# Three layer norms in two phases, with the mean's row applied before the reciprocal deviation's, and eight bridge tiles instead of seven

## The chip, the cores and the metric

The kernel runs on one core of one Trainium2 chip. The metric is the device time of one execution in microseconds (us): median of three runs before the change 1218.24 us (1216.67 to 1220.58). Besides, one execution was taken by the hardware profiler; its rows are the ones quoted here.

## What is computed

A whole network of two blocks on 256 tokens of width 1024, in float32. The first block is a mixer of a state-space branch (S5) and an mLSTM, a cross attention and a convolutional feed-forward part (FFN), with RMS norms. The second block has two layers, and it holds the layer norms of this case:

```python
def second_block(x, ...):
    alpha = (2 * DEPTH_2) ** 0.25
    for l in range(DEPTH_2):
        i = l // 2
        if l % 2 == 0:
            y = even_mixer(x, ...)
        else:
            y = odd_mixer(x, ...)
        x = layer_norm(alpha * x + y, ln_g[l, 0], ln_b[l, 0])
        y = conv_ffn(x, ffn_w_up[l], ffn_conv_w[l], ffn_conv_b[l], ffn_w_down[l])
        x = layer_norm(alpha * x + y, ln_g[l, 1], ln_b[l, 1])
    return x
```

Of its four layer norms, three feed matrix products (the FFN of the first layer, the odd mixer, the FFN of the second layer) and go through the function `layer_norm` of the kernel; the fourth is the output and has a function of its own, `last_norm`.

## The kernel before, in words

Activations lie feature-major: a tensor of [128, 8, 256] holds 1024 features as eight groups of 128 partitions, with the 256 tokens along the free axis. A matrix product of such a tensor (`fm_mm`, lines 324 to 330) makes one output tile of 128 features: for each of the eight groups three matmuls, because each float32 operand is split into a high and a low part in the reduced type float32r (high times high, high times low, low times high). So a tile is 24 matmuls of 256 columns. Each weight tile comes through `wload` (lines 312 to 322): a DMA of 512 KB into a buffer `raw`, a cast to `hi` on ScalarE (line 320), and `lo = raw - hi` on VectorE (line 321).

The sums over features that a norm needs are matmuls with a column of ones (line 454) into the one PSUM buffer of pool `pm` (tag "m"). Rows are made from such columns by `row_bcast` (lines 495 to 499): one small matmul against the identity per 128 tokens, into the same buffer "m", which ScalarE then copies to SBUF.

Since a norm takes time, TensorE is bridged. `raw_scaled` (line 526) splits z times g, not normalised, into high and low parts (`xh`, `xl`) with g and b as two more columns, and the first `NRAW` = 7 output tiles (`NROD` = 7 in the odd layer) are multiplied with that. Each such tile needs a PSUM bank for itself (258 columns): four of tag "a" and three of tag "g", which is all there is beside "m". Later `fix` (lines 1072 to 1081) corrects each tile to the product of the normalised rows: with r the reciprocal deviation and rn = -mean x r as rows, it is product x r + (W g) x rn + W b, where W g and W b are the tile's last two columns, copied by line 1076 to `wgb`. After the bridge tiles, TensorE takes the normalised rows `nh` and `nl` (in the odd layer `oh` and `ol`).

The norm itself (`layer_norm`, lines 1044 to 1064): statistics, mean and r as columns by `ln_rstd` (ScalarE lines 1035 and 1036, GpSimd lines 1038 to 1041, which ends with a power), mean x r on GpSimd (line 1050), a broadcast of r and rn in one go (line 1051), a copy of both rows on ScalarE (line 1053). Then, for five pieces of one or two groups: rn x g + b on ScalarE (line 1061), z x g x r on VectorE (line 1062), their sum (line 1063), the cast to the high part on ScalarE (line 515), the low part on VectorE (line 516).

The order of each engine's instructions is made by a scheduler that goes by priorities and a simulated timeline (`schedule_with_timeline_sim`). Norm work has `LPRI` = 600 places of priority over its place in the program, weight loads have `WPRI` = 300; `fix` and the evacuations behind it have none. Each engine then works in that fixed order and waits by semaphores.

Behind the bridge, the FFN (`ffn`, line 594) works in pairs of tiles; its PSUM tiles come from a ring of the four "a" and three "g" buffers. With seven bridge tiles the fourth pair is mixed: one bridge tile and one of normalised rows in another bank "a" (lines 363 to 384).

Of the kernel before, what the change touches and what calls it, by code (L numbers as in the profile page):

```python
# [14 lines left out]
AF = mybir.ActivationFunctionType  # L15
# [5 lines left out]
P = 128  # L21
S = 256
# [7 lines left out]
LAM_INIT = 0.8 - 0.6 * math.exp(-0.3 * 0)  # L30
MAGIC = 12582912.0
WPRI = 300
NRAW = 7
NRMS = 12
ORDER = ("kv0 ks q c0 tm ckv c1 CS0 CS1 CO0 CS2 CO1 CS3 CO2 kr CO3 cq uk uv uq DS0 DS1 DO0 DS2 DO1 DS3 "
         "DO2 DO3").split()
# [222 lines left out]
def _program(ctx, tc, nc, a, offs, dump):  # L259
    V, ACT, G, PE = nc.vector, nc.scalar, nc.gpsimd, nc.tensor  # L260
# [8 lines left out]
    tp = pool(ctx, "tp", 2)  # L269
    sm = pool(ctx, "sm", 4)  # L270
    dr = pool(ctx, "dr", 1, space=DRAM)
    pg = pool(ctx, "pg", 3, space=PSUM)
    pa = pool(ctx, "pa", 4, space=PSUM)
# [3 lines left out]
    def T(pl, shape, tag, dt=F32, **k):  # L277
        cnt[0] += 1
        return pl.tile(list(shape), dt, tag=tag, name="%s_%d" % (tag, cnt[0]), **k)

    mult, add, sub = ALU.mult, ALU.add, ALU.subtract
    stt = V.scalar_tensor_tensor
    tt = V.tensor_tensor
    ts = V.tensor_scalar
    act = ACT.activation
# [13 lines left out]
    def bc(ap, shape):  # L299
        return ap.to_broadcast(list(shape))  # L300
# [194 lines left out]
    def row_bcast(cols, at=None):  # L495
        rb = T(*(at or (pm,)), [P, len(cols) * P], "g" if at else "m")
        for j, c in enumerate(cols):
            mm(rb[:, j * P:(j + 1) * P], bc(c, [P, P]), ident, start=True, stop=True)
        return rb
# [13 lines left out]
    def split(src, h, l, scale=None):  # L513
        if scale is None:
            ACT.copy(h, src)
            tt(l, src, h, op=sub)  # L516
        else:
            act(h, src, AF.Copy, scale=scale)
            stt(l, src, scale, h, op0=mult, op1=sub)
# [68 lines left out]
    def bc2(rs):  # L588
        return bc(rs[:, None, :], [P, 2, S])

    def act_split():
        return T(hp, [P, 8, S], "xh", F32R), T(hp, [P, 8, S], "xl", F32R)
# [434 lines left out]
    def ln_stats(z):  # L1027
        with tc.high_priority(LPRI):
            st = T(pm, [P, 4], "m")
            col_sums(st, [folded(*tiles(z, 8)), folded(*squares(z, 8))])  # L1030
        return st

    def ln_rstd(st):
        nmu, mq = T(sm, [P, 2], "lnmu"), T(sm, [P, 2], "lnmq")
        act(nmu, st[:, 0:2], AF.Copy, scale=-1.0 / D)
        act(mq, st[:, 2:4], AF.Copy, scale=1.0 / D, bias=1e-5)
        var = T(sm, [P, 2], "lnv")
        G.tensor_tensor(var, nmu, nmu, op=mult)
        G.tensor_tensor(var, mq, var, op=sub)
        r = T(sm, [P, 2], "lnr")  # L1040
        G.tensor_tensor(r, var, mhalf[:, :2], op=ALU.pow)
        return nmu, r

    def layer_norm(z, g, b, h, l, xn, pl, tr_="lnrow", tf="fx"):
        st = ln_stats(z)
        raw = raw_scaled(z, g, b, S + 2)
        with tc.high_priority(LPRI):
            nmu, r = ln_rstd(st)
            nr = T(sm, [P, 2], "lnn")
            G.tensor_tensor(nr, nmu, r, op=mult)  # L1050
            rb = row_bcast([r[:, 0:1], r[:, 1:2], nr[:, 0:1], nr[:, 1:2]])
            rs = T(pl, [P, 2, S], tr_)
            ACT.copy(rs.rearrange("p a s -> p (a s)"), rb)
            rr, rn = rs[:, 0], rs[:, 1]
            for k, w in ((0, 1), (1, 1), (2, 2), (4, 2), (6, 2)):
                s2 = slice(k, k + w)
                f = T(tp, [P, w, S], "sqa", bufs=2)
                u = T(tp, [P, w, S], "sq", bufs=3)
                for n in range(w):
                    c = k + n  # L1060
                    act(f[:, n, :], rn, AF.Identity, scale=g[:, c:c + 1], bias=b[:, c:c + 1])  # L1061
                    stt(u[:, n, :], z[:, c, :], g[:, c:c + 1], rr, op0=mult, op1=mult)
                tt(xn[:, s2, :], u, f, op=add)
                split(xn[:, s2, :], h[:, s2, :], l[:, s2, :])

        places = iter([(pa, "a")] * 4 + [(pg, "g")] * 3)

        def banks(n):
            raw["tiles"] -= n
            return [T(pl_, [P, raw["n"]], tag) for pl_, tag in (next(places) for _ in range(n))]  # L1070

        def fix(rps):
            f = T(pl, [P, 2, S], tf, bufs=2)
            for n in range(len(rps)):
                wgb = T(sm, [P, 2], "wgb")
                V.tensor_copy(wgb, rps[n][:, S:S + 2])
                act(f[:, n, :], rn, AF.Identity, scale=wgb[:, 0:1], bias=wgb[:, 1:2])
                t = T(tp, [P, S], "sq", bufs=3)
                tt(t, rps[n][:, 0:S], rr, op=mult)
                tt(f[:, n, :], f[:, n, :], t, op=add)  # L1080
            return f

        raw.update(fix=fix, banks=banks, tiles=NRAW if tf == "fx" else NROD)
        return raw

    def last_norm(z):
        gb = T(hp, [P, 2, D], "xh")
        nc.scalar.dma_start(gb, bass.AP(a["ln_last"].tensor, 0, [[0, P], [D, 2], [1, D]]))
        u = T(hp, [P, 2, D], "xl")
        o = T(xp, [P, 2, D], "x")  # L1090
        st = ln_stats(z)
        zt = [[T(pa, [P, 512], "a") for q in range(2)] for t in range(2)]

        def turn(k):
            for t in range(2):
                PE.transpose(zt[t][k // 4][:, (k % 4) * P:(k % 4 + 1) * P], z[:, k, t * P:(t + 1) * P], ident)

        for k in range(6):
            turn(k)
        with tc.high_priority(LPRI):  # L1100
            nmu, r = ln_rstd(st)
        for k in range(6, 8):
            turn(k)
        for t in range(2):
            for q in range(2):
                c = slice(512 * q, 512 * q + 512)
                stt(u[:, t, c], zt[t][q], nmu[:, t:t + 1], gb[:, 0, c], op0=add, op1=mult)
        for t, c0, n in ((0, 0, 512), (0, 512, 512), (1, 0, 512), (1, 512, 256), (1, 768, 256)):
            c = slice(c0, c0 + n)
            stt(o[:, t, c], u[:, t, c], r[:, t:t + 1], gb[:, 1, c], op0=mult, op1=add)  # L1110
            nc.sync.dma_start(a["out"][t * P:(t + 1) * P, c], o[:, t, c])
# [497 lines left out]
    with ExitStack() as ph:  # L1609
# [22 lines left out]
        rs, rc = rms_defer(x, 8, C["mix_norm_g"], 1e-6, xh, xl)  # L1632
# [100 lines left out]
    h, l = act_split()  # L1733
    rs, rc = rms_defer(x3, 8, C["final_norm_g"], 1e-6, h, l)
# [10 lines left out]
    with ExitStack() as ph:  # L1745
# [12 lines left out]
        z = T(xp, [P, 8, S], "x")  # L1758
        gemm_pairs("ev_out", range(4), 6, yh, yl, join=True, **residual_a(xa, z))
    for i in range(2):  # L1760
# [4 lines left out]
        if i == 1:  # L1765
            with ExitStack() as ph:
# [6 lines left out]
                h, l = T(ap_, [P, 8, S], "oh", F32R), T(ap_, [P, 8, S], "ol", F32R)  # L1773
                raw = norm_od(h, l, ap_, "ockv", "csb0")
                yh, yl = odd(ap_, h, l, W, KO, raw)
                z = T(xp, [P, 8, S], "x")
# [3 lines left out]
        z = T(xp, [P, 8, S], "x")  # L1780
# [3 lines left out]
        if i == 0:  # L1784
            xa = T(xp, [P, 8, S], "x")
            norm_od = norm(1, z, xa)
    last_norm(z)


# [10 lines left out]
```

## Time and profile before

| what | value |
|---|---|
| median of three runs | 1218.24 us (1216.67 to 1220.58) |
| the profiled execution's own time | 1222.49 us |
| its span, first to last instruction | 1220.7 us |
| mean granted TensorE clock | 0.98 of full speed |
| busy share of the span | TensorE 96%, VectorE 74%, ScalarE 56%, GpSimd 8% |

In the profile, PE is TensorE's matmuls, PEld its weight loads, DVE is VectorE, ACT ScalarE, POOL GpSimd, SP the engine that issues most DMAs. Lines such as L321 are lines of the kernel; many operations have the line of a helper. Matmuls overlap, so a count of matmuls started in a stretch says more than the busy time of PE. PEclk is the TensorE clock that was granted: 1.00 is 2.4 GHz, 0.50 is 1.2 GHz, and a value between is a mix of both in the stretch. The three norms lie at about 660 to 702 us (first FFN), 855 to 897 us (odd mixer) and 1010 to 1047 us (second FFN).

### The profile page before, as it was taken

To read this page: it belongs to the slowest core of one execution; us is meant where nothing else is said; L and a number is where in the kernel's file an instruction comes from. 1 tells how busy PE (TensorE), PEld (TensorE's weight loads), DVE (VectorE), ACT (ScalarE), POOL (GpSimd) and SP (SyncE) were. 2 spreads that over 40 slices of the span, in tenths; PEclk is the share of its full clock that TensorE was granted. 3 is DMA by queue.
4 is the path that set the end of the run, shared out by engine and by line. 5 is a ranking of instruction groups with operands and counts; after the bars stand their busy time and mean duration, and the time that the engine had idled before them with its cause. 6 is when DMAs were issued, how large, how long until landed. Compare 5 with 4: busy or idle time off the path is not lost.

```text
span 1220.7 us, 23603 instructions
## 1 busy us (share of the span) xinstructions
PE 1175.4 (96%) x9370; PEld 1111.6 (91%) x9370; DVE 905.4 (74%) x1744; ACT 681.7 (56%) x1205; POOL 94.5 (8%) x94
## 2 busy tenths in 40 slices
PE   7779999999999999999999899999999999999997
PEld 7769989999999999899998899998977789999986
DVE  8998957866689886667564886666687758976654
ACT  5345564755566765446355675554675566755541
POOL 4830000100000000000001000001000001000010
PEclk9979999999999999999999899999998999999998
DMA  7423445664356556656423556566754215666561
GB/s 262 139 87 114 147 137 179 205 202 157 100 177 196 183 177 181 196 175 215 163 79 106 170 173 187 176 181 190 261 182 139 70 54 193 208 188 188 160 201 36
DMA packets 61276, 199.41 MB, mean 163 GB/s; under 512 B 8502, under 2 KB 12398, under 8 KB 60910
## 3 DMA queue, kind: packets, MB, share of 16 engines
q1 hardware_dynamic: 54864, 191.60, 49.5%
q10 hardware_dynamic: 6302, 6.32, 1.6%
q8 instruction: 73, 1.20, 0.4%
q14 instruction: 37, 0.30, 0.1%
HBM read 196.28 MB, written 1.60 MB: 162 GB/s over the span
## 4 chain that ended last, share of the span: by engine, by line
PE 82%; DVE 11%; ACT 2%; DMA 2%; issue 2%; SPq 0%; DVEq 0%; ACTq 0%
PE g L329 10%; PE g L328 10%; PE g L330 10%; PE a L328 7%; PE a L329 7%; PE a L330 7%; PE a L393 5%; PE g L393 4%; DVE lo L321 3%; PE a L395 3%; PE g L337 2%; PE g L339 2%; PE g L338 2%; PE g L395 2%; PE a L947 1%
## 5 line engine op out<-in xcount | busy, mean ns | idle before, releaser
L321 DVE TENSOR_TENSOR lo<-raw,hi 128x1024 fp32r<-128x1024 f32 (+3 forms) x359 | 431.2, 1206 | 180.7 <-ACT hi L320 178.0
L320 ACT CAST hi<-raw 128x1024 fp32r<-128x1024 f32 (+3 forms) x359 | 363.7, 1020 | 355.4 <-PE g L329 138.8
L328 PE MATMUL g<-xh,hi 128*128 128x256 f32 (+1 forms) x616 | 176.2, 287 | 7.9 <-ACT xh L568 7.6
L329 PE MATMUL g<-xl,hi 128*128 128x256 f32 (+1 forms) x624 | 178.9, 287 | 0.3 <-DVE xl L569 0.3
L330 PE MATMUL g<-xh,lo 128*128 128x256 f32 (+1 forms) x616 | 176.3, 287 | 2.7 <-DVE lo L321 2.7
L328 PE MATMUL a<-nh,hi 128*128 128x256 f32 x560 | 159.9, 286 | 4.6 <-ACT sqa L1061 2.7
L329 PE MATMUL a<-nl,hi 128*128 128x256 f32 x560 | 159.5, 285 | 0.9 <-DVE nl L516 0.9
L330 PE MATMUL a<-nh,lo 128*128 128x256 f32 x560 | 159.3, 285 | 0.0
L328 PEld LDWEIGHTS g<-xh,hi 128*128 128x128 f32 x616 | 117.7, 191 | 9.9 <-ACT xh L568 7.9
L330 PEld LDWEIGHTS g<-xh,lo 128*128 128x128 f32 x616 | 117.4, 191 | 4.4 <-DVE lo L321 3.4
L329 PEld LDWEIGHTS g<-xl,hi 128*128 128x128 f32 x624 | 119.0, 191 | 1.4 <-DVE xl L569 0.9
L328 PEld LDWEIGHTS a<-nh,hi 128*128 128x128 f32 x560 | 108.6, 194 | 5.7 <-ACT sqa L1061 2.9
L329 PEld LDWEIGHTS a<-nl,hi 128*128 128x128 f32 x560 | 108.7, 194 | 1.1 <-DVE nl L516 1.1
L330 PEld LDWEIGHTS a<-nh,lo 128*128 128x128 f32 x560 | 108.7, 194 | 0.0
L393 PE MATMUL a<-mx,hi 128*128 128x512 f32 x264 | 91.9, 394 | 0.0
L328 PE MATMUL g<-nh,hi 128*128 128x256 f32 x288 | 81.5, 283 | 0.0
L329 PE MATMUL g<-nl,hi 128*128 128x256 f32 x288 | 81.5, 283 | 0.0
L330 PE MATMUL g<-nh,lo 128*128 128x256 f32 x288 | 81.5, 283 | 0.0
L395 PE MATMUL a<-mx,lo 128*128 128x256 f32 x264 | 73.1, 277 | 0.0
L393 PE MATMUL g<-mx,hi 128*128 128x512 f32 x198 | 69.0, 395 | 0.0
L393 PEld LDWEIGHTS a<-mx,hi 128*128 128x128 f32 x264 | 49.4, 188 | 11.5
L328 PEld LDWEIGHTS g<-nh,hi 128*128 128x128 f32 x288 | 55.3, 192 | 0.0
(619 smaller groups left out, 2905.2 us busy)
## 6 DMA issues: line engine op xcount, KB each, us to landing
raw<-g_up SPq DMA_DIRECT2D x88, 512.0 KB, 3.6
raw<-f_up SPq DMA_DIRECT2D x44, 512.0 KB, 3.5
raw<-g_dn SPq DMA_DIRECT2D x32, 512.0 KB, 3.6
raw<-w_fm SPq DMA_DIRECT2D x27, 512.0 KB, 4.1
raw<-ev_fm SPq DMA_DIRECT2D x20, 512.0 KB, 3.7
raw<-f_dn SPq DMA_DIRECT2D x16, 512.0 KB, 3.6
raw<-od_fm SPq DMA_DIRECT2D x14, 512.0 KB, 4.2
raw<-g_dn SPq DMA_DIRECT2D x16, 384.0 KB, 3.4
```

The lines of the kernel that those rows point to most:

```text
L320: ACT.copy(hi, raw)
L321: tt(lo, raw, hi, op=sub)
L328: mm(ps, hi[:, o:o + P], xh[:, k, :], start=start and k == 0, stop=False, skip_group_check=skip)
L329: mm(ps, hi[:, o:o + P], xl[:, k, :], start=False, stop=False, skip_group_check=skip)
L330: mm(ps, lo[:, o:o + P], xh[:, k, :], start=False, stop=stop and k == kt - 1, skip_group_check=skip)
L337: mm(ps, xh[:, k, t], hi[:, wsl], start=start and j == 0, stop=False, skip_group_check=skip)
L338: mm(ps, xh[:, k, t], lo[:, wsl], start=False, stop=False, skip_group_check=skip)
L339: mm(ps, xl[:, k, t], hi[:, wsl], start=False, stop=stop and j == len(ks) - 1, skip_group_check=skip)
L393: mm(f2, hi[:, o], X[:, k].rearrange("p a s -> p (a s)"), start=first and j == 0, stop=False, skip_group_check=True)
L395: mm(ps[:, 0, :], lo[:, o], X[:, k, 0, :], start=False, stop=last and j == len(ks) - 1, skip_group_check=True)
L947: PE.transpose(tr[:, k, :], b, ident)
```

## The change

The mean's row is broadcast and copied by itself and added (as minus the mean) to z into `xn`; then the row of r is broadcast and copied, and in pairs of groups the deviation is multiplied by it, after which ScalarE makes the high part with g and b, and the normalised value is made once more in float32 (by VectorE for the first four groups, by ScalarE for the others) for the low part. The mean times r on GpSimd is gone. `fix` reads each bridge tile out of PSUM together with the mean's term (W g times minus the mean), multiplies a pair by r's row and adds W b per tile, all on VectorE. The number of bridge tiles of the two FFNs is eight; since only seven banks exist, the eighth takes the first bank "a" once more. Four corrected pairs can lie in SBUF instead of two. `ln_rstd` is split in two functions for that, and `last_norm` calls both.

```diff
-NRAW = 7
+NRAW = 8
+RB = dict(fx=4, csb0=2)
...
-    def ln_rstd(st):
-        nmu, mq = T(sm, [P, 2], "lnmu"), T(sm, [P, 2], "lnmq")
+    def ln_mean(st):
+        nmu = T(sm, [P, 2], "lnmu")
         act(nmu, st[:, 0:2], AF.Copy, scale=-1.0 / D)
+        return nmu
+
+    def ln_rstd(st, nmu):
+        mq = T(sm, [P, 2], "lnmq")
         act(mq, st[:, 2:4], AF.Copy, scale=1.0 / D, bias=1e-5)
         var = T(sm, [P, 2], "lnv")
         G.tensor_tensor(var, nmu, nmu, op=mult)
         G.tensor_tensor(var, mq, var, op=sub)
         r = T(sm, [P, 2], "lnr")
         G.tensor_tensor(r, var, mhalf[:, :2], op=ALU.pow)
-        return nmu, r
+        return r
 
     def layer_norm(z, g, b, h, l, xn, pl, tr_="lnrow", tf="fx"):
         st = ln_stats(z)
         raw = raw_scaled(z, g, b, S + 2)
         with tc.high_priority(LPRI):
-            nmu, r = ln_rstd(st)
-            nr = T(sm, [P, 2], "lnn")
-            G.tensor_tensor(nr, nmu, r, op=mult)
-            rb = row_bcast([r[:, 0:1], r[:, 1:2], nr[:, 0:1], nr[:, 1:2]])
-            rs = T(pl, [P, 2, S], tr_)
-            ACT.copy(rs.rearrange("p a s -> p (a s)"), rb)
-            rr, rn = rs[:, 0], rs[:, 1]
-            for k, w in ((0, 1), (1, 1), (2, 2), (4, 2), (6, 2)):
-                s2 = slice(k, k + w)
-                f = T(tp, [P, w, S], "sqa", bufs=2)
-                u = T(tp, [P, w, S], "sq", bufs=3)
-                for n in range(w):
+            nmu = ln_mean(st)
+            rows = T(pl, [P, 2, S], tr_)
+            rr, rm = rows[:, 0], rows[:, 1]
+            r = ln_rstd(st, nmu)
+            ACT.copy(rm, row_bcast([nmu[:, 0:1], nmu[:, 1:2]]))
+            for k in range(0, 8, 2):
+                tt(xn[:, k:k + 2, :], z[:, k:k + 2, :], bc2(rm), op=add)
+            ACT.copy(rr, row_bcast([r[:, 0:1], r[:, 1:2]]))
+            for k in range(0, 8, 2):
+                u = T(tp, [P, 2, S], "sq", bufs=3)
+                tt(u, xn[:, k:k + 2, :], bc2(rr), op=mult)
+                for n in range(2):
                     c = k + n
-                    act(f[:, n, :], rn, AF.Identity, scale=g[:, c:c + 1], bias=b[:, c:c + 1])
-                    stt(u[:, n, :], z[:, c, :], g[:, c:c + 1], rr, op0=mult, op1=mult)
-                tt(xn[:, s2, :], u, f, op=add)
-                split(xn[:, s2, :], h[:, s2, :], l[:, s2, :])
-
-        places = iter([(pa, "a")] * 4 + [(pg, "g")] * 3)
+                    gc, bc_ = g[:, c:c + 1], b[:, c:c + 1]
+                    act(h[:, c, :], u[:, n, :], AF.Identity, scale=gc, bias=bc_)
+                    if k < 4:
+                        ts(xn[:, c, :], u[:, n, :], gc, bc_, op0=mult, op1=add)
+                    else:
+                        act(xn[:, c, :], u[:, n, :], AF.Identity, scale=gc, bias=bc_)
+                tt(l[:, k:k + 2, :], xn[:, k:k + 2, :], h[:, k:k + 2, :], op=sub)
+
+        places = itertools.cycle([(pa, "a")] * 4 + [(pg, "g")] * 3)
...
         def fix(rps):
-            f = T(pl, [P, 2, S], tf, bufs=2)
-            for n in range(len(rps)):
-                wgb = T(sm, [P, 2], "wgb")
-                V.tensor_copy(wgb, rps[n][:, S:S + 2])
-                act(f[:, n, :], rn, AF.Identity, scale=wgb[:, 0:1], bias=wgb[:, 1:2])
-                t = T(tp, [P, S], "sq", bufs=3)
-                tt(t, rps[n][:, 0:S], rr, op=mult)
-                tt(f[:, n, :], f[:, n, :], t, op=add)
+            m = len(rps)
+            f = T(pl, [P, 2, S], tf, bufs=RB[tf])
+            wgb = T(sm, [P, 2, 2], "wgb", bufs=4)
+            for n in range(m):
+                V.tensor_copy(wgb[:, n], rps[n][:, S:S + 2])
+                stt(f[:, n, :], rm, wgb[:, n, 0:1], rps[n][:, 0:S], op0=mult, op1=add)
+            tt(f[:, :m, :], f[:, :m, :], bc(rr[:, None, :], [P, m, S]), op=mult)
+            for n in range(m):
+                ts(f[:, n, :], f[:, n, :], wgb[:, n, 1:2], None, op0=add)
             return f
...
         with tc.high_priority(LPRI):
-            nmu, r = ln_rstd(st)
+            nmu = ln_mean(st)
+            r = ln_rstd(st, nmu)
```

## Rows read from the trace of the kernel before

**Rows 1.** The page: busy time by engine, share of the span, instructions

```profile
PE 1175.4 (96%) x9370; PEld 1111.6 (91%) x9370; DVE 905.4 (74%) x1744; ACT 681.7 (56%) x1205; POOL 94.5 (8%) x94
```

**Rows 2.** Stretches: length, busy (x started) PE PEld DVE ACT POOL, PEclk, DMA, GB/s

```profile
690.00:702.00 12.00, 7.97 (x41) 7.46 (x40) 11.67 (x28) 8.02 (x16) 0.00 (x0) 0.72 0.34 108
706.00:718.00 12.00, 12.00 (x102) 12.00 (x101) 11.95 (x20) 9.77 (x18) 0.00 (x0) 1.00 0.61 188
1036.00:1042.00 6.00, 4.49 (x32) 3.79 (x31) 6.00 (x14) 4.73 (x8) 0.00 (x0) 1.00 0.77 263
...
908.00:924.00 16.00, 13.81 (x66) 7.75 (x65) 12.55 (x45) 12.19 (x39) 0.71 (x1) 0.57 0.52 152
...
690.00:694.00 4.00, 1.20 (x9) 0.86 (x7) 4.00 (x10) 4.00 (x10) 0.00 (x0) 1.00 0.54 179
```

**Rows 3.** TensorE's waits, whole run: in total, times, longest (us)

```profile
PE a L328 <- ACT sqa L1061: 2.7, 1, 2.7
...
PE g L454 <- ACT sq L491: 2.2, 1, 2.2
...
PE a L328 <- DVE sq L1079: 1.2, 1, 1.2
PE a L329 <- DVE nl L516: 0.9, 1, 0.9
...
PE g L337 <- DVE wgb L1076: 0.3, 1, 0.3
```

**Rows 4.** VectorE in order of time: start, length, what, [idle before]; norms 1, 2, 3

```profile
691.12 0.42 DVE L516 TENSOR_TENSOR nl<-x,nh 128x256 fp32r<-128x256 f32 x1
691.45 0.69 DVE L1063 TENSOR_TENSOR x<-sq,sqa 128x512 f32<-128x512 f32 x1
692.05 0.42 DVE L516 TENSOR_TENSOR nl<-x,nh 128x256 fp32r<-128x256 f32 x1
692.39 0.42 DVE L1079 TENSOR_TENSOR sq<-a,lnrow 128x256 f32<-128x256 f32 x1
...
698.43 0.69 DVE L516 TENSOR_TENSOR nl<-x,nh 128x512 fp32r<-128x512 f32 x1
...
876.27 1.67 DVE L1062 SCALAR_TENSOR_TENSOR sq<-x,consts,ockv 128x256 f32<-128x256 f32 x4 [0.83 <-ACT ockv L1053]
...
1044.81 0.69 DVE L516 TENSOR_TENSOR nl<-x,nh 128x512 fp32r<-128x512 f32 x1
```

**Rows 5.** TensorE, ScalarE and GpSimd in order of time, first norm

```profile
692.91 0.36 PE L328 MATMUL a<-nh,hi 128*128 128x256 f32 x1 [2.75 <-ACT sqa L1061]
...
679.36 0.17 ACT L1035 ACTIVATE lnmu<-m 128x2 f32<-128x2 f32 x1 [0.38 <-PE m L454]
...
684.19 0.58 ACT L1053 COPY lnrow<-m 128x512 f32<-128x512 f32 x1 [1.37 <-PE m L498]
...
689.84 1.09 ACT L1061 ACTIVATE sqa<-lnrow,consts 128x256 f32<-128x256 f32 x2
...
681.43 0.82 POOL L1050 TENSOR_TENSOR lnn<-lnmu,lnr 128x2 f32<-128x2 f32 x1
```

**Rows 6.** Stretches as in rows 2: first and third norm, the first FFN behind

```profile
680.00:700.00 20.00, 15.97 (x114) 15.42 (x113) 19.23 (x43) 15.22 (x27) 2.01 (x4) 0.87 0.60 184
...
1026.00:1046.00 20.00, 18.49 (x150) 17.79 (x149) 19.98 (x40) 15.49 (x26) 1.22 (x2) 1.00 0.67 237
...
704.00:820.00 116.00, 116.00 (x927) 113.91 (x926) 82.85 (x132) 67.54 (x109) 0.00 (x0) 1.00 0.59 181
```

**Rows 7.** VectorE by line and shape, from 400 us on: busy, mean ns | idle before

```profile
L605 DVE SCALAR_TENSOR_TENSOR cv<-a,consts,cv 128x254 f32<-128x254 f32 x43 | 20.2, 478 | 0.1
...
L1484 DVE TENSOR_SCALAR csb<-csb,cden 128x256 f32<-128x256 f32 x16 | 4.6, 350 | 0.0
```

**Rows 8.** The chain of waits, odd layer: start, length, what

```profile
900.26 7.97 DMA raw<-od_fm
```

## Prediction

> **What bounds the kernel now.** I read the page's busy shares first: TensorE is busy 96% of the span, VectorE 74%, ScalarE 56% [rows 1]. So time can be won only where TensorE waits or runs slow. Next the table of stretches. 12 us at full rate start 102 matmuls (0.118 us each); 690 to 702, where the first layer norm feeds the FFN, starts 41, so (102 - 41) x 0.118 = 7.2 us are lost there. The third norm (1036 to 1042) starts 32 where 6 us at full rate start 51: 19 x 0.118 = 2.2 us. At the odd layer's norm TensorE waits 0.3 us [rows 2, 3]. That is 9.7 us, 0.8% of the span: all that a better layer norm can win directly.
>
> The waits say why. In the first norm TensorE waits 2.7 us for its first tile on normalised rows and 1.2 us more at the next [rows 3]. The first wait ends at 692.91, although that tile's first rows were complete at 691.54 [rows 4, 5]. The tile writes a PSUM buffer "a", of which there are four, all held by bridge tiles (products of unnormalised z, corrected later), and the first correction to read one ends at 692.81 [rows 4]. The second wait ends as another such read ends. So PSUM was late, because the correction needs the reciprocal deviation and queues on VectorE behind the norm. In the third norm the longest wait is 0.9 us, for a low part [rows 3]. **The clock** adds to this: TensorE starts 9 matmuls from 690 to 694, and over 690 to 702 its granted clock is 0.72, against 1.00 before and after [rows 2]. With levels of 1.00 (2.4 GHz) and 0.50 (1.2 GHz) that is 12 x 0.28 / 0.5 = 6.7 us at half, so up to 3.4 of the 7.2 us lost. In the third norm it stayed at 1.00.
>
> VectorE is behind both: busy 19.2 of 20 us in the first norm and 20.0 in the third, ScalarE 15 in each [rows 6].
>
> **The change, part by part.** Costs are start-to-start times on VectorE: 0.60 us for a two-input operation on 512 values (691.45 to 692.05), 0.34 on 256 (692.05 to 692.39), 0.42 for the fused one on 256 (four in 1.67) [rows 4]. The fused one lasts 0.48 reading PSUM, and tensor_scalar on 256 lasts 0.35 [rows 7]; taking off the 0.08 by which others overlap (0.42 to 0.34), they are 0.40 to 0.42 and 0.27. ScalarE takes 0.5 per 256 (two in 1.09) [rows 5].
>
> *Statistics to rows.* The first norm's mean is on ScalarE at 679.36; the row copy starts at 684.19 and takes 0.58 [rows 5]. The change drops GpSimd's mean-times-r (0.82 here), halves the broadcast that has r, and its copy. The mean's row needs no GpSimd result and goes ahead. The second broadcast reuses the one PSUM tile "m" and so waits for the copy of the first; behind it on TensorE's queue stand bridge matmuls, but that copy should be over before r is. I take r's row to be there 1.5 us earlier (0.8, and 0.7 of the 2.5 us from GpSimd's end at 682.25 to the copy's end), at 683.3.
>
> *The norm on VectorE.* Before, all after r: 8 x 0.42 + 2 x (2 x 0.34 + 3 x 0.60) = 8.3 us. After: 4 x 0.60 = 2.4 us ahead of r, then 4 x 0.60 (times r) + 4 x 0.27 + 4 x 0.60 (low parts) = 5.9 us. The total is the same; 2.4 us move forward. *On ScalarE* a copy of 512, eight scalings and eight groups' casts become two copies of 256 and twelve scalings: about 6.5 us both times.
>
> *The correction.* Per tile before: product and sum on VectorE, 0.68, and 0.5 on ScalarE. After: fused read of PSUM 0.42, half a 512-wide product 0.30, sum with a scalar 0.27: 0.99, none on ScalarE (the two-value copy is in both). With eight tiles instead of seven VectorE goes from 4.8 to 7.9 us, ScalarE from 3.5 to nothing. The fused read needs only the mean's row, so a bank can leave some 4 us sooner if VectorE has time for it. The added 3.1 us can wait, as four corrected pairs now fit in SBUF instead of two. Their cover is the FFN behind, where VectorE is busy 82.9 of 116 us with TensorE at full rate [rows 6]; if that cover is gone, late evacuations hold PSUM and the 3.1 us come back as waits. A rule of the Trainium skill speaks against this part: "VectorE: DVE Perf Modes", Rules for kernel authors, says to minimise the number of Vector operations. Per FFN norm they go from 39 to 44; the sums here go by durations and hold more than that.
>
> *The eighth tile* is 24 matmuls (2.8 us) that no longer need the norm: TensorE's bridge, which ended at 690.2 (692.91 less the wait), reaches 693.0.
>
> **The sum.** Before, the norm's last low part ended at 699.1 [rows 4], 14.3 us after the row: 8.3 of its own and 6.0 that slipped between. After: 683.3 + 5.9 + 6.0 + 1.7 (four fused reads) = 696.9. TensorE, starting on rows at 693.0, wants the last pair 2.1 us on (three pairs of groups, six matmuls each), at 695.1. So 1.8 us stay lost, and I take it that the clock stays up, as it did in the third norm with 2.2 us lost: the first norm gains **5.4**. In the third, the last low part ended at 1045.5 [rows 4]; the bridge ended about 1037.2, so that was 6.2 us after it was wanted, and it cost 2.2. The same steps make that about 2 us, which in proportion costs 0.7: gain **1.5**.
>
> *The odd norm* keeps seven tiles and TensorE there is covered, but VectorE carries 7 x 0.69 + 3 x 0.60 + 0.34 - 4.8 = 2.2 us more. The chain of waits runs through that VectorE stretch into a weight load that lands late, 7.97 us after its issue; then a wait of 2.2 us for a square, and 908 to 924 at a granted clock of 0.57 [rows 2, 3, 8]. The trace does not price a shift of this chain. Bounds: all of it goes (2.2 + 0.43 x 16 = 9 us gained), or the 2.2 us are added with as much again at half clock (4.4 us lost). VectorE idles 0.83 us just before this norm's rows come [rows 4], which the mean's adds can fill; I take 2.2 - 0.8 = 1.4 **lost**, nearest to that row.
>
> -5.4 - 1.5 + 1.4 = **-5.5 us**. The profiled execution took 1222.49 (span 1220.7 and 1.8 around it), 4.25 above the median of the runs, 1218.24. It becomes 1217.0, and the median **1212.7**.
>
> **Rivals.** (a) *VectorE sets the pace.* It had under 1 us free in 20, and its own norm work is unchanged in total; the weights' low parts and the fused reads stand in the same queue. Then the last low part comes at 699 again, and only the bank wait and part of the clock go, half of the first norm's 7.2: -3.6 in the first, nothing in the third, +1.4 in the odd: 1216.0, within 0.3%. For it: 20.0 of 20 busy [rows 6]. Against it: the bank's release moves even so, and 2.4 us of the norm run before r. Also here: the gain is real and the odd chain takes it back. Chance 0.24.
> (b) *Slower: the clock falls in the third norm as well.* The reads that release banks have no priority; on a full VectorE they come behind norm and weights, later than now. TensorE runs out at tile eight in both norms, and each loses 7.2: +5.0 in the third, nothing won in the first: 1223.2. It decides if the third norm's stretch comes to look as 690 to 694 does now, just ahead of the fall [rows 2]. Against it: that read's operands are ready before the reciprocal deviation, and the third norm kept its clock with 2.2 us lost. A rule of the Trainium skill would make it likelier: "TensorE: Matmul & The Clock Gate", A second HAM failure mode, tells of kernels that cycle through PSUM banks and idle in short steps until the clock swings between its levels. By that rule the third norm should have dropped already; the trace disagrees at that amount. With the odd chain's 4.4 us this case reaches 1228. Chance 0.14.
> (c) *It does more*: all 9.7 us go: 1208.5, and with a little of the odd chain's 9 some 1207. Chance 0.12.
> (d) *It doesn't do what it says*: the order within each engine is made by a simulated timeline, and the fused reads could stay behind the weights; that is case (a).
>
> **How the numbers follow.** The forecast has 0.50, (a) 0.24, (b) 0.14, (c) 0.12. A measurement of this kernel tells about 0.3% (3.7 us) from no change, so faster means below 1214.6: the forecast and (c), 0.62; (a) is the same, 0.24; slower 0.14. The range runs from 1207 (all of (c)) to 1220 (past (a), with 0.14 left above).
>
> **What would show it.** Right: the first norm's stretch starts 85 or more matmuls in 12 us with the clock at 1.00; no wait of TensorE on a correction's read of "a"; eight bridge tiles; a row of the mean some microseconds ahead of r's; ScalarE freer, VectorE still full. Wrong step by step: last low part at 699 or later (VectorE's pace), a bank wait that only moved (the reads' order), a clock of 0.5 in the third norm (b), or a longer stretch at 0.57 in the odd layer. If the norms' stalls close and the time stays, the odd chain took it.

## The result: slower, with the profile after

The changed kernel takes 1228.58 us (median of four runs, 1228.18 to 1232.95) against 1217.53 for the kernel before in the same comparison: a ratio of 1.0093, 95% interval 1.0076 to 1.0111. The forecast was 1212.7, the range ended at 1220. The profiled execution took 1232.95 (span 1231.2), 4.4 above its median, much as the one of before was 4.25 above its own, so the two spans can be set side by side: +10.5 us.

Cut at the statistics of the norms (the mean on ScalarE, line 1036 now; other lines moved by 1 to 10), that difference lies as follows: 1.0 before the first norm, 2.0 from there to the odd norm (191.45 to 193.42), 4.2 in the odd layer (153.85 to 158.02), 3.4 from the third norm to the end. These are single executions; how far they scatter is told in part 3 of the experiments.

Waits of TensorE in the changed kernel, first for 680 to 712 us (first norm), then for 1030 to 1065 (third):

```profile
PE a L330 <- DVE nl L1072: 3.9, 1, 3.9
PE a L329 <- ACT hi L321: 2.8, 1, 2.8
...
PE a L330 <- DVE nl L1072: 1.7, 2, 1.2
PE a L329 <- ACT hi L321: 0.9, 1, 0.9
```

Against [rows 3], the wait for a PSUM bank (a correction's read of "a") is gone, as forecast. In its place stand two waits. One is for the norm's low parts `nl` (3.9 us in the first norm, 1.7 in the third). The other is for the high part of a weight (2.8 and 0.9), whose cast in the first norm stands on ScalarE, without idle time between, behind eight scalings of the norm:

```profile
691.98 2.57 ACT L1067 ACTIVATE nh<-sq,consts 128x256 fp32r<-128x256 f32 x5
...
695.93 1.03 ACT L321 CAST hi<-raw 128x1024 fp32r<-128x1024 f32 x1
```

Together they are 6.7 us in the first norm, against 3.9 for banks before.

The stretches that answer to [rows 2] (us, PE busy with matmuls started, granted clock, DMA share, GB/s):

```profile
694.00:706.00 12.00, 5.29 (x25) 0.60 0.42 131
...
1048.00:1052.00 4.00, 1.97 (x13) 0.92 0.89 330
1052.00:1056.00 4.00, 3.47 (x16) 0.50 0.60 200
1056.00:1060.00 4.00, 4.00 (x27) 0.72 0.42 130
```

In the first norm 25 matmuls start in 12 us where 102 could: (102 - 25) x 0.118 = 9.1 us lost, 1.9 more than before. In the third, 52 start from 1048 to 1060 (a matmul that runs over the border of two stretches is counted in both, so the three counts add up to 56): (102 - 52) x 0.118 = 5.9 lost, 3.7 more, and now the clock falls there too. These two terms are about the 2.0 and the 3.4 of the spans.

Why the low parts are late, in the timeline of the first norm (start, us, engine, line, operation, idle time ahead of it). First the broadcasts of the mean and of r on TensorE:

```profile
682.86 0.60 PE L499 MATMUL m<-consts,lnmu 128*128 128x128 f32 x4
686.54 0.61 PE L499 MATMUL m<-consts,lnr 128*128 128x128 f32 x4
```

On ScalarE the mean's column and the copies of both rows:

```profile
680.34 0.17 ACT L1036 ACTIVATE lnmu<-m 128x2 f32<-128x2 f32 x1 [0.39 <-PE m L455]
...
683.70 0.36 ACT L1057 COPY lnrow<-m 128x256 f32<-128x256 f32 x1
...
687.19 0.37 ACT L1060 COPY lnrow<-m 128x256 f32<-128x256 f32 x1 [1.30 <-PE m L499]
```

And r itself on GpSimd:

```profile
681.62 0.71 POOL L1046 TENSOR_TENSOR lnr<-lnv,mhalf 128x2 f32<-128x2 f32 x1
```

r was done at 682.33 and its buffer "m" free at 684.06, but its broadcast stands in TensorE's queue behind bridge matmuls until 686.54. So r's row came 7.2 us after the statistics (687.56 - 680.34), where it took 5.4 before and I had forecast 3.9.

Then VectorE from r's row to the last low part (same columns):

```profile
687.82 1.65 DVE L1086 SCALAR_TENSOR_TENSOR fx<-lnrow,wgb,a 128x256 f32<-128x256 f32 x4
...
689.45 1.21 DVE L322 TENSOR_TENSOR lo<-raw,hi 128x1024 fp32r<-128x1024 f32 x1
690.59 1.89 DVE L1063 TENSOR_TENSOR sq<-x,lnrow 128x512 f32<-128x512 f32 x3
...
692.46 1.21 DVE L322 TENSOR_TENSOR lo<-raw,hi 128x1024 fp32r<-128x1024 f32 x1
693.60 1.28 DVE L1087 TENSOR_TENSOR fx<-fx,lnrow 128x512 f32<-128x512 f32 x2
694.80 0.47 DVE L1086 SCALAR_TENSOR_TENSOR fx<-lnrow,wgb,g 128x256 f32<-128x256 f32 x1
...
695.26 0.72 DVE L1069 TENSOR_SCALAR x<-sq,consts 128x256 f32<-128x256 f32 x2
695.90 1.21 DVE L322 TENSOR_TENSOR lo<-raw,hi 128x1024 fp32r<-128x1024 f32 x1
697.04 0.73 DVE L1069 TENSOR_SCALAR x<-sq,consts 128x256 f32<-128x256 f32 x2
697.68 0.47 DVE L1086 SCALAR_TENSOR_TENSOR fx<-lnrow,wgb,g 128x256 f32<-128x256 f32 x1
...
698.15 1.13 DVE L1089 TENSOR_SCALAR fx<-fx,wgb 128x256 f32<-128x256 f32 x4
699.19 0.47 DVE L1086 SCALAR_TENSOR_TENSOR fx<-lnrow,wgb,g 128x256 f32<-128x256 f32 x1
699.59 0.68 DVE L1072 TENSOR_TENSOR nl<-x,nh 128x512 fp32r<-128x512 f32 x1
700.19 0.68 DVE L1063 TENSOR_TENSOR sq<-x,lnrow 128x512 f32<-128x512 f32 x1
700.79 0.68 DVE L1072 TENSOR_TENSOR nl<-x,nh 128x512 fp32r<-128x512 f32 x1
701.39 1.21 DVE L322 TENSOR_TENSOR lo<-raw,hi 128x1024 fp32r<-128x1024 f32 x1
...
702.69 0.68 DVE L1072 TENSOR_TENSOR nl<-x,nh 128x512 fp32r<-128x512 f32 x1
703.30 0.68 DVE L1087 TENSOR_TENSOR fx<-fx,lnrow 128x512 f32<-128x512 f32 x1
703.90 0.47 DVE L1086 SCALAR_TENSOR_TENSOR fx<-lnrow,wgb,a 128x256 f32<-128x256 f32 x1
...
705.08 0.68 DVE L1072 TENSOR_TENSOR nl<-x,nh 128x512 fp32r<-128x512 f32 x1
```

VectorE has no idle time here, and it takes up the products with r's row (L1063) only at 690.59, 3.0 us after that row, behind four reads of banks and a weight's low part. The first low part starts 19.25 us after the statistics; before it was 11.76 (691.12 less 679.36, [rows 4, 5]). Between r's row and the end of the last low part lie 18.2 us, by start-to-start times: norm 6.2, corrections 6.0 (reads L1086, pair products L1087, sums L1089), low parts of weights 4 x 1.14 = 4.6, the rest 1.4. Before, not one operation that corrects a tile stood ahead of the second low part (the first read of a bank was at 692.39, behind `nl` at 691.12 and 692.05, [rows 4]); now 13 stand ahead of the first (the small copies to `wgb` not counted).

### The profile page after: what moved, and what is told of

Its sections match the earlier page's. It is cut to its first block, busy times and chain, and to the rows that moved or that the text cites. A ratio compares the mean times of both kernels' runs of the same rounds, so it can differ in the third digit from the quotient of the medians.

```text
span 1231.2 us, 23578 instructions
## 1 busy us (share of the span) xinstructions
PE 1178.4 (96%) x9370; PEld 1117.8 (91%) x9370; DVE 914.3 (74%) x1756; ACT 672.0 (55%) x1184; POOL 88.7 (7%) x91
## 4 chain that ended last, share of the span: by engine, by line
PE 88%; DVE 7%; ACT 2%; issue 1%; DMA 1%; DVEq 0%; POOL 0%; SPq 0%; ACTq 0%
PE g L330 12%; PE g L329 12%; PE g L331 12%; PE a L330 7%; PE a L331 7%; PE a L329 7%; PE a L394 5%; PE g L394 4%; PE a L396 3%; PE g L340 2%; PE g L339 2%; PE g L338 2%; PE g L396 2%; DVE lo L322 2%; PE a L948 1%
## 5 line engine op out<-in xcount | busy, mean ns | idle before, releaser
L330 PE MATMUL a<-nl,hi 128*128 128x256 f32 x544 | 155.9, 287 | 5.6 <-DVE nl L1072 5.6
L329 PE MATMUL a<-nh,hi 128*128 128x256 f32 x544 | 155.5, 287 | 3.6 <-ACT hi L321 3.6
L331 PE MATMUL a<-nh,lo 128*128 128x256 f32 x544 | 155.5, 286 | 0.0
L330 PEld LDWEIGHTS a<-nl,hi 128*128 128x128 f32 x544 | 105.5, 194 | 6.4 <-DVE nl L1072 6.4
L329 PEld LDWEIGHTS a<-nh,hi 128*128 128x128 f32 x544 | 105.4, 194 | 4.0 <-ACT hi L321 4.0
L331 PEld LDWEIGHTS a<-nh,lo 128*128 128x128 f32 x544 | 105.5, 194 | 0.0
L396 PE MATMUL g<-mx,lo 128*128 128x256 f32 x198 | 55.4, 282 | 0.0
```

What stands on the lines that cost most here:

```text
L329: mm(ps, hi[:, o:o + P], xh[:, k, :], start=start and k == 0, stop=False, skip_group_check=skip)
L330: mm(ps, hi[:, o:o + P], xl[:, k, :], start=False, stop=False, skip_group_check=skip)
L331: mm(ps, lo[:, o:o + P], xh[:, k, :], start=False, stop=stop and k == kt - 1, skip_group_check=skip)
L396: mm(ps[:, 0, :], lo[:, o], X[:, k, 0, :], start=False, stop=last and j == len(ks) - 1, skip_group_check=True)
```

## The experiments

Each was compared with the kernel before on the chip that it ran on. Rows_once to odd_old shared one chip, newnorm_oldfix to old_eight_read a second, corr_last_once to odd_newfix a third, and new_corr_last had a fourth; the kernel before had medians of 1216.2 to 1218.5 us there. So between runs of different chips the ratios say more than the microseconds, which can be 1 to 2 us off. "Odd old" means that the odd layer has the norm and correction of before; the FFN parts are then compared without it. The low-part columns are microseconds after the first norm's statistics, from each profile.

| run | FFN norm / correction, tiles | odd layer | us | ratio (95% interval) | first, last low part |
|---|---|---|---|---|---|
| the change | new / new, 8 | new | 1228.6 | 1.0093 (1.0076 to 1.0111) | 19.3, ends 25.4 |
| rows_once | new, rows together / new, 8 | new, rows together | 1225.9 | 1.0063 (1.0042 to 1.0085) | 20.7, 26.3 |
| new_seven | new / new, 7 | new | 1237.1 | 1.0150 (1.0121 to 1.0179) | 19.3, 24.7 |
| old_eight | old / old, 8 | old | 1213.3 | 0.9961 (0.9946 to 0.9975) | 11.8, 19.7 |
| odd_old | new / new, 8 | old | 1223.0 | 1.0040 (1.0019 to 1.0061) | 19.3, 25.4 |
| newnorm_oldfix | new / old, 8 | old | 1216.2 | 0.9996 (0.9978 to 1.0014) | 13.1, 20.0 |
| oldnorm_newfix | old / new, 8 | old | 1225.4 | 1.0070 (1.0047 to 1.0092) | 17.1, 27.3 |
| corr_last | as odd_old, other order | old | 1212.4 | 0.9963 (0.9947 to 0.9978) | 15.8, 20.2 |
| old_eight_read | old / old, first reads early, 8 | old | 1213.2 | 0.9969 (0.9952 to 0.9986) | 13.1, 22.8 |
| corr_last_once | corr_last, rows together | old | 1214.8 | 0.9978 (0.9960 to 0.9996) | 16.1, 20.5 |
| odd_newnorm | corr_last | new norm, old correction | 1215.9 | 0.9981 (0.9963 to 0.9999) | 15.8, 20.2 |
| odd_newfix | corr_last | old norm, new correction | 1217.2 | 0.9993 (0.9978 to 1.0008) | 15.8, 20.2 |
| new_corr_last | corr_last | new | 1218.2 | 1.0003 (0.9982 to 1.0023) | 15.8, 20.2 |

**1. Is it r's late row, or the eighth tile, or the odd layer?** My theory after reading the profile was the late row (theory 1), with the order on VectorE as its rival (theory 2).

```diff
-            ACT.copy(rm, row_bcast([nmu[:, 0:1], nmu[:, 1:2]]))
+            rb = row_bcast([r[:, 0:1], r[:, 1:2], nmu[:, 0:1], nmu[:, 1:2]])
+            ACT.copy(rows.rearrange("p a s -> p (a s)"), rb)
...
-            ACT.copy(rr, row_bcast([r[:, 0:1], r[:, 1:2]]))
```

> The changed kernel with one edit: minus the mean and r are broadcast together in one PSUM tile and copied together (512 values), as the kernel before did it, and the adds of the mean follow that copy. Theory 1 (r's row late): in the changed kernel the second broadcast stood on TensorE behind bridge matmuls until 686.54 although r was done at 682.33, so r's row came 7.2 us after the statistics against 5.4 before. Then r's row comes about 2 us sooner, the low parts with it, and the time falls by 4 to 8 us, to 1221 to 1225. Theory 2 (the corrections' operations stand ahead of the norm's low parts on VectorE): the 2.4 us of adds now stand behind r's row, nothing else moves, and the time stays within 2 us of 1228.6. Theory 3 (the eighth bridge tile): same as theory 2.

The copy of both rows on ScalarE (the mean's column was at 680.27), then the first low part on VectorE:

```profile
685.08 0.59 ACT L1058 COPY lnrow<-m 128x512 f32<-128x512 f32 x1 [1.36 <-PE m L499]
```

```profile
700.95 0.68 DVE L1072 TENSOR_TENSOR nl<-x,nh 128x512 fp32r<-128x512 f32 x1
```

r's row came 1.8 us sooner, as meant, and the first low part 1.4 us later. The time fell by 2.7 us, between the two theories, with intervals that overlap. The low parts decide the reading for the FFNs: the row was not what held them. TensorE waits 7.1 us in the first norm's stretch, 6.7 in the changed kernel. No run has r's row as early as forecast (3.9 us) with the mean's adds ahead of it.

```diff
-NRAW = 8
+NRAW = 7
```

> The changed kernel with seven bridge tiles in the FFNs instead of eight. Theory 1 (r's row late): the rows come as late as with eight, and TensorE wants them 2.8 us sooner in two norms, so it is slower by up to 5 us: 1229 to 1234. Theory 2 (corrections ahead of the low parts): one correction less, 1.0 us of VectorE, in each FFN, against 2.8 us less of bridge: 1228 to 1232. Theory 3 (the eighth tile, which must wait for a bank that a correction frees and puts its own weight and correction before the low parts, is what costs): faster by 3 us or more, below 1225.6.

It is 8.6 us slower than with eight (6.9 by the ratios), more than any of the three had: TensorE waits 8.2 and 1.7 us in the first norm (3.9 and 2.8 with eight). The eighth tile is a gain, and theory 3 falls. The same tile in the kernel before:

```diff
-NRAW = 7
+NRAW = 8
...
-        places = iter([(pa, "a")] * 4 + [(pg, "g")] * 3)
+        places = itertools.cycle([(pa, "a")] * 4 + [(pg, "g")] * 3)
```

> The kernel before with one edit: eight bridge tiles in the FFNs, the eighth taking the first bank of tag a once more; norm and correction as before. Theory 3 (the eighth tile costs): slower than 1217.5 by 3 us or more. Theories 1 and 2: its own correction still needs r and comes as late as before, so TensorE waits for the bank at the eighth tile as it did at the first tile on normalised rows (2.7 us), and the rows are wanted 2.8 us later: within 3 us of 1217.5, rather below it.

0.9961: that alone makes the kernel before 4.7 us faster, more than its expectation had. The bank wait has only moved to the eighth tile (2.8 us). So without the eighth tile the rest of the change costs 1.5%, some 19 us (new_seven).

For `odd_old` the changed kernel calls the old `layer_norm` wherever it is given the odd layer's tags:

```diff
-            return lambda h, l, pl, *tags: layer_norm(zt, g, b, h, l, xn, pl, *tags)
+            return lambda h, l, pl, *tags: (layer_norm_old if tags else layer_norm)(zt, g, b, h, l, xn, pl, *tags)
```

> The changed kernel with the old norm and the old correction in the odd layer alone; both FFNs as changed. By the spans of the profiled executions the odd norm and mixer took 158.0 us against 153.9 before, so the odd layer is 4.2 of the 11 us: 1224.4. If the two norms of the FFNs are the whole cause (the odd stretch differs only by what it inherits): within 1.5 us of 1228.6. If the odd chain is the main cause: 1221 or less.

1223.0: the odd layer costs 5.6 us (6.5 by the ratios, whose intervals don't touch). What is left above the kernel before, 0.4%, is the FFNs'.

**2. Norm or correction, and amount or order?** Theory A: the new correction stands ahead of the low parts. Theory B: the two-phase norm is itself late. For the first run the old `fix` (with four buffers) stands behind the new norm, and mean times r is made again; for the second, the new `fix` behind the old norm, with a row of the mean copied ahead.

```diff
+            nr = T(sm, [P, 2], "lnn")
+            G.tensor_tensor(nr, nmu, r, op=mult)
...
-            ACT.copy(rr, row_bcast([r[:, 0:1], r[:, 1:2]]))
+            ACT.copy(rows[:, 0:2].rearrange("p a s -> p (a s)"),
+                     row_bcast([r[:, 0:1], r[:, 1:2], nr[:, 0:1], nr[:, 1:2]]))
...
-                stt(f[:, n, :], rm, wgb[:, n, 0:1], rps[n][:, 0:S], op0=mult, op1=add)
...
+                act(f[:, n, :], rn, AF.Identity, scale=wgb[:, 0:1], bias=wgb[:, 1:2])
...
+                tt(t, rps[n][:, 0:S], rr, op=mult)
...
```

> FFNs with the two-phase norm and eight bridge tiles but the old correction (product with r on VectorE, sum with a row made on ScalarE; mean times r is made again for it and comes with r's row); the odd layer as before the change. It lies between odd_old (new norm, new correction: 1223.0) and old_eight (old norm, old correction: 1213.3). Theory A (the new correction crowds in ahead of the norm's low parts): the first low part comes under 17 us after the statistics instead of 19.3, and the time is 1213 to 1217. Theory B (the two-phase norm itself is late: second broadcast, deviation and normalised value one after the other): the first low part stays at 18 us or later, and the time is 1220 to 1224.

```diff
+            rm = T(pl, [P, S], "lnrm")
+            ACT.copy(rm, row_bcast([nmu[:, 0:1], nmu[:, 1:2]]))
...
```

> FFNs with the old norm and eight bridge tiles but the new correction (fused read with the mean's row, product of a pair, sum with W b, all on VectorE; the mean's row is broadcast and copied ahead for it); the odd layer as before the change. Between old_eight (1213.3) and odd_old (1223.0). Theory A (the correction crowds in): the first low part is 3 us or more later than old_eight's 11.8 us after the statistics, and the time is 1218 to 1222. Theory B (the two-phase norm): the low parts come as in old_eight, the wait of 2.8 us for the bank of the eighth tile is gone, and the time is 1209 to 1214.

With the old correction the two-phase norm has its first low part at 13.1 us, although its r row came later still (7.9 us), and takes 1216.2. That is still above old_eight (0.9996 against 0.9961, intervals apart): TensorE waits 4.1 us in the first norm for a bank of "a", whose read by the old correction needs r's row. With the new correction the old norm has it at 17.1 and takes 1225.4. VectorE of the second run ahead of that low part:

```profile
686.07 1.29 DVE L1097 TENSOR_TENSOR fx<-fx,lnrow 128x512 f32<-128x512 f32 x2
...
689.22 1.14 DVE L1099 TENSOR_SCALAR fx<-fx,wgb 128x256 f32<-128x256 f32 x4
...
693.38 0.42 DVE L517 TENSOR_TENSOR nl<-x,nh 128x256 fp32r<-128x256 f32 x1
```

The same products and sums again stand ahead of `nl`. Of its 5.3 us of lateness against old_eight, though, 2.5 are its row (7.9 us against 5.4), so this run overstates the correction. Theory A has the better of it; the next run takes the order alone:

```diff
-                tt(l[:, k:k + 2, :], xn[:, k:k + 2, :], h[:, k:k + 2, :], op=sub)
+                last = V.tensor_tensor(l[:, k:k + 2, :], xn[:, k:k + 2, :], h[:, k:k + 2, :], op=sub)
...
-                stt(f[:, n, :], rm, wgb[:, n, 0:1], rps[n][:, 0:S], op0=mult, op1=add)
-            tt(f[:, :m, :], f[:, :m, :], bc(rr[:, None, :], [P, m, S]), op=mult)
-            for n in range(m):
-                ts(f[:, n, :], f[:, n, :], wgb[:, n, 1:2], None, op0=add)
+                with tc.issue_after(last.ins) if raw["tiles"] < 4 else ExitStack():
+                    stt(f[:, n, :], rm, wgb[:, n, 0:1], rps[n][:, 0:S], op0=mult, op1=add)
+            with tc.issue_after(last.ins):
+                tt(f[:, :m, :], f[:, :m, :], bc(rr[:, None, :], [P, m, S]), op=mult)
+                for n in range(m):
+                    ts(f[:, n, :], f[:, n, :], wgb[:, n, 1:2], None, op0=add)
```

(`issue_after` sets the place in the engine's queue and adds no wait.)

> odd_old (new norm, new correction, eight tiles; odd layer as before) with the same operations in another order: in the FFNs the corrections' pair products, sums with W b, and the fused reads of the third and fourth pair are issued on VectorE behind the norm's last low part. That moves 3 products, 4 sums and 4 reads (some 4.5 us) behind. Theory A: the low parts come 3 to 5 us sooner and TensorE waits that much less in each FFN norm: 1214 to 1218. Theory B: the low parts are held by the norm's own steps and by ScalarE, under 2 us are won: 1221 to 1225.

VectorE's queue around the low parts, then TensorE's waits from 680 to 712 us:

```profile
692.76 0.68 DVE L1072 TENSOR_TENSOR nl<-x,nh 128x512 fp32r<-128x512 f32 x1
...
696.47 0.69 DVE L1072 TENSOR_TENSOR nl<-x,nh 128x512 fp32r<-128x512 f32 x1
697.07 1.29 DVE L1089 TENSOR_TENSOR fx<-fx,lnrow 128x512 f32<-128x512 f32 x2
698.27 1.26 DVE L1087 SCALAR_TENSOR_TENSOR fx<-lnrow,wgb,g 128x256 f32<-128x256 f32 x3
```

```profile
PE a L329 <- ACT hi L321: 2.8, 1, 2.8
```

With the same operations, the first low part (692.76) is 3.4 us sooner after the statistics (676.94 here) than in odd_old, the last ends 5.2 sooner, at 20.2, and the products and reads follow it. Only the four reads of the "a" banks are left ahead of the first low part. TensorE's wait for low parts in the first norm is gone; 2.8 us remain, for the high part of a weight on ScalarE (no run changed the order there). The time is 1212.4 against 1223.0, with intervals that don't touch. This is the cause in the FFNs: the order, 10.6 us of it by the medians and 9.4 by the ratios. In the two profiles 8.5 us of the difference lie between the first norm and the odd one and from the third norm to the end. The version also beats both kernels, but it only draws level with old_eight (0.9961): in no order tried here did the new norm and correction win anything beside the eighth tile.

**3. What is left over, and the rest of the change.** In old_eight the bank wait of 2.8 us remained, so its first two reads were put ahead of the norm:

```diff
+                if tf == "fx" and raw["tiles"] == NRAW - 2:
+                    t = T(pl, [P, S], "fxq", bufs=2)
+                    with tc.high_priority(3000):
+                        tt(t, rps[n][:, 0:S], rr, op=mult)
...
```

> old_eight with one edit: in the FFNs the products of the first pair of bridge tiles with r (the reads that free two banks of tag a) go to a buffer of their own and stand on VectorE ahead of the norm's products. In old_eight the eighth tile waited 2.8 us for that read in the first norm, and the clock was 0.62 in the 4 us after. If that wait is what is left: 2 to 4 us faster than old_eight, 1209 to 1211.5. If the 0.8 us that the norm gives up comes back as a later low part: within 1 us of 1213.3.

No gain: of the bank wait 0.4 us is left, but the last low part ends 3.1 us later (22.8 for 19.7), and TensorE waits for low and high parts instead (1.8 us in three waits). In VectorE's full stretch, what was put ahead of the low parts here cost what it won.

Then the place of r's row, now that the order is mended: the edit of rows_once, in the FFNs of corr_last.

> corr_last (1212.4) with minus the mean and r broadcast together and copied in one go in the FFNs, so that r's row comes 5.4 us after the statistics instead of 7.2, and the adds of the mean behind it. If r's row coming late was itself a cost, now that the corrections no longer stand ahead of the low parts: 2 to 4 us faster, 1208 to 1210.5. If it was not (the adds fill the time until r's row, and the row's place counts little): within 1.5 us of 1212.4, or slower by up to 2 us.

1214.8, not distinguishable from corr_last (the intervals overlap), and certainly not faster by 2 to 4. The row is 1.8 us sooner, the adds stand behind it, the first low part is at 16.1 instead of 15.8. By the first low part, the mean going ahead and r's row coming late about cancel.

Last the odd layer, with corr_last in the FFNs; the layer has the old norm's code with one half exchanged, as in the two runs of part 2.

> corr_last in the FFNs (1212.4 with the odd layer as before the change), and in the odd layer the two-phase norm with the old correction. The change of the whole odd layer cost 5 us (odd_old against the changed kernel: 1228.6 less 1223.0). If it is the norm (r's row 1.6 us later, and the first corrected tiles that the mixer's chain starts from wait for it): 1215 to 1218. If it is the correction: within 1.5 us of 1212.4.

> corr_last in the FFNs (1212.4), and in the odd layer the old norm with the new correction, all of it on VectorE. If the odd layer's 5 us come from the correction (2.2 us more of VectorE work, which stands ahead of the mixer's own chain): 1214.5 to 1218. If they come from the two-phase norm: within 1.5 us of 1212.4.

The norm alone gives 0.9981 and the correction alone 0.9993, against 0.9963 for neither: 2 and 4 us by the ratios, both with intervals that overlap or touch their neighbour's. Which half weighs more is not settled. The profiles don't settle it either: the odd layer spans 148.0 to 153.9 us with unchanged code in eight profiles, and with the new code 158.0 in the changed kernel, 160.1 in new_seven, 152.3 in new_corr_last and 152.0 in rows_once (rows together). So the 4.2 us of the spans above measure little by themselves. In the changed kernel's odd layer (863 to 1018 us) TensorE has five waits, the longest

```profile
PE g L329 <- DVE xh L1554: 3.1, 1, 3.1
...
```

and the other four 1.0 to 1.1 each, over the mixer's own chain: 7.4 us in all, against the 2.2 for a square of [rows 3] and 2.0 in three smaller groups before. The same code in new_corr_last waits 4.1 us there, and not for `xh`. That the new code costs the odd layer some 5 us is shown by the medians; by which wait is open.

And the changed kernel whole, with nothing but the FFNs' order altered:

> The changed kernel itself, odd layer included, with nothing but the order on VectorE in the two FFNs altered as in corr_last. If the order costs the FFNs 10.6 us (odd_old 1223.0 to corr_last 1212.4) and the odd layer's 5 us stand beside it: 1228.6 less 10.6 is 1218, that is 1216 to 1220, no slower than the kernel before. If the two hang together (the odd layer's loss is inherited from a late first FFN): 1211 to 1214.5. If corr_last won only because the odd layer was the old one: 1222 or more.

1218.2, a ratio of 1.0003: as the first reading had it. By the ratios the order is worth 11.0 us here (1.0093 to 1.0003). It explains the loss in the FFNs, and the odd layer stands beside it.

## Why the prediction was wrong

The step that failed is the last term of the sum for the first norm, "683.3 + 5.9 + 6.0 + 1.7 (four fused reads)": I let four reads of the correction stand ahead of the low parts and said that "the added 3.1 us can wait". They could, but in the order that VectorE was given they did not. The second term that failed is "683.3", r's row. Set against what was measured, from the statistics to the end of the last low part (corr_last has the order that the forecast assumed, four reads ahead):

| term | forecast | the change | corr_last |
|---|---|---|---|
| r's row | 3.9 | 7.2 | 7.2 |
| norm behind it | 5.9 | 6.2 | 6.2 |
| corrections among it | 1.7 | 6.0 | 1.6 |
| weights' low parts and the rest | 6.0 | 6.0 | 5.2 |
| sum | 17.5 | 25.4 | 20.2 |

That the 6.0 came out is luck. I took it over from before, where it held three low parts of weights (3.4) and 2.3 us of the old correction, which the change replaces:

```profile
693.32 0.43 DVE L1080 TENSOR_TENSOR fx<-fx,sq 128x256 f32<-128x256 f32 x1
...
694.96 0.76 DVE L1079 TENSOR_TENSOR sq<-a,lnrow 128x256 f32<-128x256 f32 x2
...
697.42 0.77 DVE L1080 TENSOR_TENSOR fx<-fx,sq 128x256 f32<-128x256 f32 x2
698.09 0.43 DVE L1079 TENSOR_TENSOR sq<-a,lnrow 128x256 f32<-128x256 f32 x1
```

(and the read at 692.39 of [rows 4]). Now it is four low parts of weights and 1.4 us of small operations. With the forecast's order the changed kernel takes 1218.2 (new_corr_last): inside the range, but level with the kernel before, since the odd layer takes back what the FFNs win.

- *r's row 1.5 us sooner*: wrong, 1.8 later. I saw that the second broadcast shares "m" and that bridge matmuls stand behind the first, but priced only the wait for the buffer, not the place in TensorE's queue. Of the loss it explains little (rows_once, corr_last_once): against a row at 5.4 it only gave back the 2.4 us of adds that went ahead.
- *The correction's price*, 0.99 us per tile on VectorE: right (0.39 for a read, 0.60 for a pair's product, 0.26 for a sum, start to start). Its place was wrong. The old correction's read needs r's row, as the norm's own products do, and in old_eight_read it went ahead of them only with a priority of its own; the new read needs only the mean's row. Why the scheduler now put products and sums of the correction, too, ahead of work with 600 places of priority was not looked into.
- *The bank comes free sooner*: right. All four "a" banks were read by 689.4, and no wait for one is left in the FFNs.
- *The eighth tile*, 2.8 us per FFN: right in sign. With both FFNs 5.6 us were expected; it gave 8.6 in the changed kernel (6.9 by the ratios) and 4.7 in the old.
- *The clock stays up*: wrong in consequence. TensorE ran dry, its granted clock was 0.60 from 694 to 706 us, and in the third norm it fell to 0.50.
- *The odd layer loses 1.4*: right in sign, too small; the runs give about 5 (odd_old 5.6; corr_last against new_corr_last 0.4%), past even the bound of 4.4. A shift of its chain was the one thing the trace of before did not price, and I took a value well inside the bounds.
- *Rivals.* (a), VectorE sets the pace, names the mechanism, but I let its loss end where the old low parts had been. (b) named the falling clock in the third norm and was closest in time (1223 to 1228), but by late reads of banks, which did not occur.

The Trainium skill's rule in "VectorE: DVE Perf Modes", Rules for kernel authors, to minimise the number of operations, pointed the right way for the change as it stood. Yet corr_last has the same operations as odd_old and is 10.6 us faster (9.4 by the ratios): here their place counted more than their number.

## What to carry to other kernels

When an engine is full around a handover, write down its queue in order and sum what stands ahead of the operation that the next engine waits for; that a piece of work *can* wait says nothing until its place is known. Do the same for each engine that hands over: once VectorE's order was mended, a cast on ScalarE was the longest wait of the first norm. Work that becomes ready sooner may also be issued sooner, so making a side task independent can push the main task back; pin it behind with an order constraint. And test the cheap part alone: eight bridge tiles without the rest gave as much (0.9961) as the whole FFN change in its best order (0.9963).

## What was not expected of the hardware

The same stall need not cost the same clock. corr_last and odd_newfix have the same order of instructions on TensorE and VectorE around the first norm, and each waits 2.8 us there, for the same weight. Four stretches of each, from the same point after the statistics (corr_last first):

```profile
688.00:692.00 4.00, 2.82 (x24) 1.00 0.52 152
692.00:696.00 4.00, 2.37 (x19) 1.00 0.72 246
696.00:700.00 4.00, 4.00 (x36) 1.00 0.43 131
700.00:704.00 4.00, 4.00 (x35) 1.00 0.00 0
```

```profile
688.75:692.75 4.00, 2.82 (x24) 1.00 0.60 163
692.75:696.75 4.00, 2.34 (x16) 0.89 0.73 235
696.75:700.75 4.00, 4.00 (x26) 0.69 0.41 131
700.75:704.75 4.00, 4.00 (x36) 1.00 0.00 0
```

In one the clock stays at 1.00 (2.4 GHz); in the other it falls towards 0.50 (1.2 GHz) after the wait, with 0.89 and 0.69 as the means of two stretches, and is back at 1.00 in the fourth. Over the 16 us, 98 matmuls start instead of 110 (the stretches' counts add up to 4 more), or 12 x 0.118 = 1.4 us. odd_newnorm and new_corr_last, with the same FFN order, dropped as well. Why the same stall costs the clock in three profiles and not in the fourth is open. A single profile can thus be 1.4 us off on one such stall, which is as much as the smaller effects here, and more elsewhere: corr_last and new_corr_last, with the same code up to there, reach the first norm's statistics at 676.94 and 680.41 us. So those effects are judged by medians of several runs.
